# A 4096 x 4096 Strassen-like matmul on one core: the fourth product of seven regions in quarters, and A's rows measured on ScalarE

## The chip, the cores and the metric

The kernel runs on one core of a Trainium2 chip. The metric is the device time of one execution in microseconds (us); lower is better. The core's engines each follow their own instruction list in order: TensorE (PE in the profile; its weight loads are PEld), VectorE (DVE), ScalarE (ACT), GpSimd (POOL) and SyncE (SP). POOL, SP and ACT also issue DMA transfers.

## What is computed

```python
def reference(a, b, alpha):          # a, b: 4096 x 4096 float32, alpha = 0.01
    x = np.matmul(a, b)
    return np.where(x > 0, x, alpha * x)
```

The kernel multiplies in float16 with float32 sums and replaces eight block products by seven, in the manner of Strassen and Winograd. Because the sums of blocks lose accuracy where rows of A or columns of B differ much in size, it also sums the squares of every row of A and every column of B ("measures" them). At the end it looks at the largest, the smallest and the total, and a plain branch in bfloat16 computes the product again if they are too uneven. On this input that branch isn't taken.

## The kernel before, in words

The output is cut into 4 bands `g` of 1024 rows and 4 column blocks `j` of 1024 columns; one pair is a **region**, named (g, j) here. The first region, (0,0), is computed plainly while the first data come in; the other 15 follow in the list `regions` (L487), in a band in the order 2, 0, 1, 3 (band 2: 2, 0, 3, 1; band 0: 1, 2, 3). In each, A's band and B's block are split into halves (A11 to A22, B11 to B22), and seven products of 512 x 2048 by 2048 x 512 are made. `PRODUCTS` (L622) lists them: a11, a12, s2, s3, s1, a22 and s4 are the left sides, where s1 to s4 are sums of A's blocks, made once a band. The right sides are B11, B21, T2, T3, T1, T4 and B22: VectorE makes the T's in place with `b_sum` (L569, eight of 128x4096 a region). T3 lies where B12 was, T2 and T1 where B11 was.

A whole product (`product`, L725; matmuls on L734) is 64 matmuls of 512 columns into four PSUM banks. In the ten regions of bands 1 to 3 that are not the last of a band that another band follows (`in_quarters`, L901), the sixth and the seventh product use the same scheme again one level down: seven products of a quarter each (`quarter_product`, L678, matmuls on L684), 16 matmuls of 256 columns. They need four sums of quarters of A (`sums_of_a`, made in the first region of a band, stored in DRAM and loaded in the others by `load_sums`) and four of B (`t3_of_b` and `sums_of_b`, L644 to L656, on VectorE). Of the four quarters of the left side, the third, x[1,0], is used only in such sums, never as an operand.

Around the products the order is written by hand; the text of the loop is each engine's order. In a region it is: product 0; `early.end`; the middle measure begins; `keep` copies product 0's banks to SBUF by ScalarE (L747); the four `b_sum`s for T3 and T2, with a small memset (L702) after which SP reloads the second half of s2; the middle measure ends; product 1 and its `add` (L869) and `leave` (leaky pass L307, stores L874); four `b_sum`s for T4 and T1; product 2, its `keep`, the late measures; product 3 and its `keep` into `v`; then T3 and sums for the sixth product, product 4, and so on. As `v` takes the buffers that the first block had, its copies wait for that block's stores.

A `Measure` (L212) squares four pieces of 128x2048 with ScalarE (L227) into buffers of the pool `a16` (three buffers), and VectorE adds, turns, reduces and folds them into `stats` (L236 to L260). Which block is measured where stands in `MEASURED` and `EARLY` (L611, L620). The fields of `MEASURED` are the middle measure, the late ones and two more.

B's blocks are fetched by POOL as converting DMAs (L513; column block 2 is kept in float16 and loaded by SP), each into the place of the same block of the region before, as soon as TensorE has released it: B12 after product 3, B11 after product 4, B21 in the sixth product, B22 after the seventh. In the last region of bands 0 to 2 (`turning`) the next band of A comes in: `fetch_a` (L889) has POOL fetch 16 pieces of 128 rows into `a16` buffers (L130), and VectorE turns each (`turn`, L139).

Of the kernel before, what the change touches and what calls it, by code (L numbers as in the profile page):

```python
# [8 lines left out]
P = 128  # L9
DT = mybir.dt.float16  # L10
BF16 = mybir.dt.bfloat16
# [35 lines left out]
def kernel(  # L47
# [4 lines left out]
    alpha,  # L52
    out: bass.AP,
):

# [63 lines left out]
    def load_a(row, k0, kw, tiles, to, dt=DT):  # L121

        kc = kw // P
        held = []

        def fetch():
            a16 = a16_pool.tile([P, 4 * tiles, kw // 4], dt, name="a16")
            for q in range(4):
                src = a[row:row + tiles * P, k0 + q * kw // 4:k0 + (q + 1) * kw // 4]
                nc.gpsimd.dma_start(a16[32 * q:32 * q + 32], src.rearrange("(g i) w -> i g w", i=32))  # L130
            held.append(a16)

        def turn(t0=0, t1=tiles):
            parts = to(t0, t1)
            n = kc // 2 // len(parts)
            src = (held[0][:, 4 * t0:4 * t1, :].rearrange("p g w -> p (g w)").bitcast(U32)
                   .rearrange("p (g j c) -> p g c j", j=32, c=kc // 2))
            for i, part in enumerate(parts):
                nc.vector.transpose(  # L139
                    part.rearrange("p c m e -> p c (m e)").bitcast(U32)  # L140
                    .rearrange("p c (g i) -> p g c i", i=32),
                    src[:, :, i * n:(i + 1) * n, :],
                )

        return fetch, turn

    def pieces_a(g, h, u, urgent=False):
# [423 lines left out]
    def measure(i, which, x, y, room=None):  # L571
# [7 lines left out]
            return MeasureFirst(which, parts, None)  # L579
        return Measure(which, parts, not which, room)  # L580

    def judge(line):


        ends = small_pool.tile([P, 3, 2], FP32, name="ends")
        for n, op in enumerate((MAX, MIN, ADD)):
            nc.vector.tensor_reduce(ends[:, n], stats[:, n], axis=X, op=op)
        lines = dram_pool.tile([P, 6], FP32, name="lines")
        nc.sync.dma_start(lines, ends.rearrange("p n w -> p (n w)"))
        nc.sync.dma_start(line, lines.rearrange("p k -> (p k)").rearrange("(o k) -> o k", o=1))  # L590
        yield
        by = line.rearrange("o (p n w) -> o n w p", n=3, w=2)
        most, least, total, ok, more = (
            small_pool.tile([1, 2], FP32, name=name) for name in ("most", "least", "total", "ok", "more"))
        for t, n, op in ((most, 0, MAX), (least, 1, MIN), (total, 2, ADD)):
            nc.vector.tensor_reduce(t, by[:, n], axis=X, op=op)
        nc.vector.tensor_scalar(more, least, EVEN, None, op0=MULT)
        nc.vector.tensor_tensor(ok, most, more, LE)
        for t, limit, op in ((most, GREATEST, LE), (least, LEAST, GE), (total, 1e30, LE)):
            nc.vector.tensor_scalar(more, t, limit, None, op0=op)  # L600
            nc.vector.tensor_tensor(ok, ok, more, MULT)
        good = small_pool.tile([1, 1], I32, name="good")
        nc.vector.tensor_tensor(good, ok[:, :1], ok[:, 1:], MULT)
        yield good
# [3 lines left out]

    A11, A12, A22 = (0, 0, 0), (0, 0, 1), (0, 1, 1)
    B11, B12, B21, B22 = ((1, half, nt) for half in range(2) for nt in range(2))  # L610
    MEASURED = {  # L611
        (0, 1): (None, [A11], B12, B11), (0, 2): (B21, [B22, A22], B12, A12),
        (1, 0): (A12, [B22], None, None), (1, 1): (A22, [A11], None, None),
        (2, 0): (B21, [A12], None, None), (2, 3): (A22, [A11], None, None),
        (3, 0): (A12, [A22], None, None),
        (3, 1): (B21, [B22], None, None), (3, 3): (B21, [B22], None, None),
    }


    EARLY = {(1, 1): B11, (2, 0): B11, (2, 3): B11, (3, 0): B12, (3, 1): B12, (3, 3): A11}  # L620

    PRODUCTS = [("a11", 0, 0), ("a12", 1, 0), ("s2", 0, 0), ("s3", 0, 1), ("s1", 0, 0), ("a22", 1, 0), ("s4", 1, 1)]  # L622


    HALF = NT // 2
    QUARTER = KC * HALF
    kept_s2 = dram_pool.tile([2, P, KC * RM], DT, name="kept_s2")
    kept_q = {name: dram_pool.tile([4, P, QUARTER], DT, name=f"kept_q{name}") for name in ("a22", "s4")}
    side = 0

    def a_quarter(t):
# [26 lines left out]
    def sums_of_a(g, name, room):  # L658

        x = {key: q.rearrange("p c m e -> p c (m e)") for key, q in quarters_of_a(g, name).items()}  # L660
        made = {}

        def make(n, x0, x1, op):
            made[n] = room(n)
            f = lambda t: made[t].rearrange("p (c m) -> p c m", m=2 * HALF) if isinstance(t, int) else x[t]
            nc.vector.tensor_tensor(f(n), f(x0), f(x1), op)
            nc.sync.dma_start(kept_q[name][n - 1], made[n])

        make(1, (1, 0), (1, 1), ADD)
        make(2, 1, (0, 0), SUB)  # L670
        make(3, (0, 0), (1, 0), SUB)
        make(4, (0, 1), 2, SUB)

    def load_sums(name, to, which, queue=nc.sync):
        for n in which:
            queue.dma_start(to[n], kept_q[name][n - 1])
# [18 lines left out]
    def new_a16(_=None):  # L695
        return a16_pool.tile([P, QUARTER], DT, name="q16", tag="a16")
# [18 lines left out]
    for i, (g, j) in enumerate(regions):  # L715
# [28 lines left out]
        def keep(banks, side):  # L744
            pairs, kept = new_c(side)
            for mt in range(MT):
                nc.scalar.copy(kept[mt], banks[mt])  # L747
            return pairs, kept

        def sixth_in_quarters(pairs, banks, v, y, tq, sq):  # L750

# [135 lines left out]
                    coming[h, half] = next_a(g + 1, h, half)  # L887

        def fetch_a(h, half, some=slice(None)):  # L889
            if turning:  # L890
                for fetch, turn in coming[h, half][some]:
                    fetch()
                    turn()

        y = [new_bank(ybank + mt) for mt in range(MT)]
        z = [new_bank(zbank + mt) for mt in range(MT)]
# [2 lines left out]
        late_ones = [measure(i, *x) for x in late_ones]  # L899
        first_of_group = i == 0 or regions[i - 1][0] != g  # L900
        in_quarters = g > 0 and not turning  # L901
        early = measure(i, *EARLY[g, j]) if (g, j) in EARLY else None
        if early:
            early.begin()
        if first_of_group and g:
            keep_s2(g)

        product(0, y, True)
        if early:
            early.end()  # L910
        if middle:
            middle.begin()
        have_t2 = g > 1 and j == CACHED
        if have_t2:
            for k in ks:
                t = have_b[i, k, 0] = b_pool.tile([P, KC, NT], DT, name="b", tag="b11")
                move_t("t2", t, k, False, nc.scalar)
        _, u1 = keep(y, side)
        for k in ks:
            if have_t2:  # L920
                break
            b_sum(B(0, 1, k), B(1, 1, k), B(0, 1, k), SUB)
            if late_s2 and k == ks[0]:
                load_s2(g, ks[1], True)
            b_sum(B(0, 0, k), B(0, 1, k), B(0, 0, k), ADD)
            if g == 1 and j == CACHED:
                move_t("t3", B(0, 1, k), k, True)
                move_t("t2", B(0, 0, k), k, True)
        if middle:
            middle.end()  # L930
        if first_of_group:
            sum_a(g, "s3")
            if g:
                sum_a(g, "s4")
# [4 lines left out]
        leave(u1, 0, 0)  # L939
        if g:  # L940
            fetch_a(0, 0, slice(3, None))
        for k in ks:
            b_sum(B(1, 0, k), B(1, 0, k), B(0, 0, k), SUB)
        if first_of_group and g:
            sums_of_a(g, "s4", new_a16)
        if not g:
            fetch_a(0, 1)

# [5 lines left out]
            b_sum(B(0, 0, k), B(1, 1, k), B(0, 0, k), SUB)  # L954
        if g:
            fetch_a(0, 1)
        if i == 0:
            sum_a(g, "s4")
        if late_ones:
            late_ones[0].end()  # L960
        if in_quarters:
            t = x_pool.tile([P, 4, QUARTER], DT, name="q", tag="x")
            tq, sq = {2: t[:, 0], 1: t[:, 1], 4: t[:, 2]}, {4: t[:, 3]}
        if in_quarters and first_of_group:
            sums_of_a(g, "a22", lambda n: sq.setdefault(n, sq[4] if n == 4 else new_a16()))
        elif in_quarters:
            for n in (1, 2, 3):
                sq[n] = new_a16()
            load_sums("a22", sq, (1, 2, 3, 4))

        z = [new_bank(zbank + mt) for mt in range(MT)]
        product(3, z, True)
        _, v = keep(z, side)
        fetch_b(i + 1, [(0, 1)], ks)
        fetch_a(1, 0)
        for m in late_ones[1:]:
            m.begin()
            m.end()
# [10 lines left out]
                good = next(judged)  # L989

        product(4, y, False)
        a21 = None
        if turning:
            new_s(g + 1, "s1")
            t = new_s(g + 1, "s2").rearrange("p k c m e -> p (k c m e)").bitcast(BF16)
            a21 = measure(i + 1, 0, 1, 0, t.rearrange("p (n w) -> p n w", n=4))
            a21.begin()
        if in_quarters:
            tq, sq = sixth_in_quarters(u2_pairs, [new_bank(zbank + mt) for mt in range(MT)], v, y, tq, sq)
        else:  # L1000
            add(v, y)
            leave(v, 1, 1)
        if a21:
            a21.end()
        if fifth:
            fifth = measure(i + 1, *fifth)
            fifth.begin()
# [105 lines left out]
```

## Time and profile before

| | |
|---|---|
| median of 3 runs | 1552.65 us (1552.44 to 1552.97) |
| the profiled execution | 1552.24 us, of which its span, first to last instruction, is 1550.1 us |
| TensorE busy (share of the span) | 1537.9 us (99%) |
| VectorE | 1154.6 us (74%) |
| ScalarE | 374.2 us (24%) |
| GpSimd | 300.4 us (19%) |
| DMA moved | 329.68 MB, mean 213 GB/s |
| granted TensorE clock, mean | 0.998 |
| chain of work that ended last | PE 96%, DMA 2%, DVE 1%, POOL 1%, issue 1% |

A busy share is a mean over stages; TensorE's 99% says that it has nearly always a matmul under way, not which wait would end last if the others changed. That is read from the timelines of single regions. In the lists, `x4` counts instructions, `[1.62 <-ACT c L819]` is the idle time of that engine before them and what ended it, and the DMA share is the busy time of the 16 DMA engines over the stretch (transfers overlap in one engine, so it can exceed 1).

### The profile page before, as it was taken

Reading aid. Unit: us, or ns where it says so; the run is one execution under the profiler, and the core shown is the slowest. Engines: PE = TensorE matmul, PEld = TensorE weight load, DVE = VectorE, ACT = ScalarE, POOL = GpSimd, SP = SyncE. Lnnn points to the kernel's source line nnn. Section 1 sums busy time; section 2 is a strip of 40 time slices with the busy share of each in tenths; the row PEclk is TensorE's granted clock in tenths of the full one; section 3 lists DMA queues with packets and bytes.
Section 4 is the critical chain, followed back from the end, with each engine's and each line's share of the span. In section 5 each row is a group of like instructions: output and inputs, shape, how many; then the busy total and the mean of one; then the engine's idle time right before and its main releaser. Section 6 shows DMA issues by size and latency. Waiting matters only on the chain.

```text
span 1550.1 us, 20720 instructions
## 1 busy us (share of the span) xinstructions
PE 1537.9 (99%) x8235; PEld 804.8 (52%) x8235; DVE 1154.6 (74%) x1315; ACT 374.2 (24%) x394; POOL 300.4 (19%) x482
## 2 busy tenths in 40 slices
PE   9999999999999999999999999999999999999997
PEld 4444444444447456474444746547444464745646
DVE  4368758777996586966699588685879769678696
ACT  2201243612110324300121141430021143051430
POOL 5641110144002011023400202012340110201100
PEclk9999999999999999999999999999999999999999
DMA  9999694999869889499996959969998894969923
GB/s 246 186 216 194 135 286 153 181 202 192 271 253 259 188 177 277 113 273 219 184 339 207 270 141 229 233 145 278 215 213 314 198 277 101 276 166 193 287 82 139
DMA packets 210092, 329.68 MB, mean 213 GB/s; under 512 B 18497, under 2 KB 155969, under 8 KB 202050
## 3 DMA queue, kind: packets, MB, share of 16 engines
q0 software_dynamic: 149376, 141.59, 57.4%
q1 hardware_dynamic: 53986, 161.12, 27.9%
q10 hardware_dynamic: 6624, 25.56, 4.4%
q8 instruction: 66, 1.08, 0.3%
q14 instruction: 40, 0.33, 0.1%
HBM read 369.10 MB, written 98.57 MB: 302 GB/s over the span
## 4 chain that ended last, share of the span: by engine, by line
PE 96%; DMA 2%; DVE 1%; POOL 1%; issue 1%; ACT 0%; SPq 0%; DVEq 0%
PE ps L734 76%; PE ps L684 16%; PE ps L279 4%; DMA b<-in_b_dram 1%; DVE a L139 1%; DMA a<-in_a_dram 0%; POOL a L130 0%; DMA a_in<-in_a_dram 0%; POOL b L189 0%; DVE part L318 0%; PE turned L366 0%; DVE part L314 0%; DVE c L860 0%; DVE c L307 0%; DVE a L373 0%
## 5 line engine op out<-in xcount | busy, mean ns | idle before, releaser
L734 PE MATMUL ps<-b,a 128*128 128x512 f16 x3200 | 696.4, 379 | 0.0
L734 PEld LDWEIGHTS <-a 128*128 128x128 f16 x3200 | 313.2, 98 | 375.6
L734 PE MATMUL ps<-b,s 128*128 128x512 f16 x2240 | 489.2, 379 | 0.0
L734 PEld LDWEIGHTS <-s 128*128 128x128 f16 x2240 | 219.1, 98 | 264.3
L513 POOL DMA_DIRECT2D b<-in_b_dram x184 | 136.6, 747 | 927.3 <-PE ps L734 582.9
L569 DVE TENSOR_TENSOR b<-b 128x4096 f16<-128x4096 f16 x104 | 234.7, 2289 | 91.3 <-DMA b<-in_b_dram 88.1
L747 ACT COPY c<-ps 128x512 f32<-128x512 f32 x180 | 92.7, 598 | 457.0 <-PE ps L734 381.9
L139 DVE STREAM_TRANSPOSE a<-a 128x512 uint32<-128x512 uint32 (+2 forms) x120 | 126.8, 1103 | 82.4 <-DMA a<-in_a_dram 79.7
L130 POOL DMA_DIRECT2D a<-in_a_dram x252 | 137.8, 553 | 196.2 <-DVE a L139 112.6
L307 DVE SCALAR_TENSOR_TENSOR c<-c 128x512 f32<-128x512 f32 x240 | 149.6, 687 | 3.1 <-ACT c L1042 3.0
L227 ACT ACTIVATE sq<-b 128x2048 bf16<-128x2048 f16 x64 | 119.2, 1911 | 107.5 <-DVE sq L236 91.1
L869 DVE TENSOR_TENSOR c<-ps,c 128x512 f32<-128x512 f32 x142 | 88.8, 682 | 67.7 <-PE ps L734 57.5
L684 PEld LDWEIGHTS <-q 128*128 128x128 f16 x1280 | 125.2, 98 | 14.5
L279 PE MATMUL ps<-b,a 128*128 128x512 f16 x512 | 112.9, 379 | 2.0 <-DVE part L318 0.9
L227 ACT ACTIVATE sq<-a 128x2048 bf16<-128x2048 f16 x48 | 89.1, 1911 | 102.2 <-DVE sq L236 81.0
L279 PEld LDWEIGHTS <-a 128*128 128x128 f16 x512 | 49.7, 98 | 63.1 <-issue 3.4
L684 PE MATMUL ps<-b,q 128*128 128x256 f16 x640 | 74.8, 273 | 0.0
L810 ACT COPY c<-ps 128x512 f32<-128x512 f32 x9 | 5.3, 588 | 253.1 <-PE ps L684 225.0
L763 DVE TENSOR_TENSOR c<-ps,c 128x512 f32<-128x512 f32 x80 | 52.3, 686 | 14.5 <-PE ps L684 14.5
L684 PE MATMUL ps<-q,q 128*128 128x256 f16 x480 | 57.3, 273 | 0.0
L684 PEld LDWEIGHTS <-a 128*128 128x128 f16 x480 | 47.0, 98 | 7.6
L684 PEld LDWEIGHTS <-s 128*128 128x128 f16 x480 | 47.0, 98 | 5.4
(100 smaller groups left out, 769.7 us busy)
## 6 DMA issues: line engine op xcount, KB each, us to landing
b<-in_b_dram POOLq DMA_DIRECT2D x192, 512.0 KB, 13.1
out_dram<-c SPq DMA_DIRECT2D x240, 256.0 KB, 6.2
a<-in_a_dram POOLq DMA_DIRECT2D x244, 128.0 KB, 5.4
b<-kept SPq DMA_DIRECT2D x20, 1024.0 KB, 8.7
q<-kept_qs ACTq DMA_DIRECT2D x40, 512.0 KB, 8.2
s<-kept_s SPq DMA_DIRECT2D x18, 1024.0 KB, 7.3
q<-kept_qa SPq DMA_DIRECT2D x28, 512.0 KB, 6.0
b<-in_b_dram POOLq DMA_DIRECT2D x24, 256.0 KB, 9.1
```

What stands on the lines that cost most here:

```text
L130: nc.gpsimd.dma_start(a16[32 * q:32 * q + 32], src.rearrange("(g i) w -> i g w", i=32))
L139: nc.vector.transpose(part.rearrange("p c m e -> p c (m e)").bitcast(U32) .rearrange("p c (g i) -> p g c i", i=32), src[:, :, i * n:(i + 1 ...
L227: nc.scalar.activation(to, self.parts[n], SQUARE)
L279: nc.tensor.matmul(ps, a_cols(at[0, h, u], c, mt, (h, u) == (0, 0)), bt[0, u, nt][:, c, :], start=first, stop=last,)
L307: nc.vector.scalar_tensor_tensor(t, t, alpha, t, op0=MULT, op1=MAX if alpha <= 1 else MIN)
L513: nc.gpsimd.dma_start(t[:, c:c + 4, :], b_rows(j, u, c, 4, nt, g > 0))
L569: nc.vector.tensor_tensor(f(to), f(x0), f(x1), op)
L684: nc.tensor.matmul(to[m], xq[:, c // 2, rows, c % 2], yq[:, c, :], start=first and c == 0 and m < banks, stop=c == KC - 1, skip_group_chec ...
L734: nc.tensor.matmul(banks[mt], a_cols(t, c, mt, t is first_a), B(half, nt, k)[:, c, :], start=first and (k, c) == todo[0], stop=(k, c) == t ...
L747: nc.scalar.copy(kept[mt], banks[mt])
L763: nc.vector.tensor_add(block, pair(t), block)
L869: nc.vector.tensor_add(to, bank, to)
```

## The change

In seven regions, all those in quarters but the first of a band (`in_fourth`), the fourth product (index 3, s3 times T3) is made in quarters too. Its sums of B's quarters are made by VectorE before the second pair of `b_sum`s. Its sums of A's quarters are made in the second region of a band (`sums_of_s3`) and lie where the quarters x[1,0] of a22, s4 and s3 were (`x21`), with the third of them in the `q` tile. They are also stored in DRAM, and loaded again in the third and fourth region. The displaced quarters are stored in DRAM (`keep_x21`, bands 1 and 2) and brought back in the turning region, where the whole products need them (`load_x21`).

The blocks of A in bands 1 to 3 are no longer measured by `Measure`. As each piece comes in, ScalarE squares its four strips and sums along them (`square_rows`), and VectorE folds 16 numbers a block into `stats` (`note_rows`). The measures of B that remain are placed anew; the middle measure now begins after `keep`. The core of the diff:

```diff
+    def square_rows(piece, n, to):
+        for q in range(4):
+            nc.scalar.activation(junk, piece[:, q, :], SQUARE, accum_out=to[:, 4 * n + q:4 * n + q + 1])
+    def note_rows(but=0):
+        while len(rows_made) > but:
+            r = rows_made.pop(0)
+            for n, op in enumerate((MAX, MIN, ADD)):
+                nc.vector.tensor_tensor(stats[:, n, 0], stats[:, n, 0], r, op)
...
+    EARLY = {(1, 0): B11, (1, 1): B11, (2, 0): B12, (2, 3): B11, (3, 1): B12}
...
-        (1, 0): (A12, [B22], None, None), (1, 1): (A22, [A11], None, None),
-        (2, 0): (B21, [A12], None, None), (2, 3): (A22, [A11], None, None),
-        (3, 0): (A12, [A22], None, None),
-        (3, 1): (B21, [B22], None, None), (3, 3): (B21, [B22], None, None),
+        (1, 1): (B21, [], None, None), (2, 0): (B22, [], None, None),
+        (3, 0): (B21, [], None, None), (3, 3): (B21, [], None, None),
     }
-    EARLY = {(1, 1): B11, (2, 0): B11, (2, 3): B11, (3, 0): B12, (3, 1): B12, (3, 3): A11}
+    IN_ROOM = {(1, 3): B22, (2, 1): B22}
...
+    def x21(g, name):
+        return operand(g, name, 0)[:, :, HALF:, :]
+    def keep_x21(g, name):
+        if g < G - 1:
+            nc.sync.dma_start(by_chunk(kept_x21[name]), by_chunk(x21(g, name)))
+    def load_x21(room, kept):
+        for c in range(KC // 2):
+            nc.sync.dma_start(by_chunk(room)[:, c], by_chunk(kept)[:, c])
+    def sums_of_s3(g, rooms):
+        x = {key: by_chunk(q) for key, q in quarters_of_a(g, "s3").items()}
+        sx = {n: by_chunk(room) for n, room in rooms.items()}
+        sx[3] = by_chunk(new_a16())
+        for n, x0, x1, op in ((1, x[1, 0], x[1, 1], ADD), (3, x[0, 0], x[1, 0], SUB),
+                              (2, sx[1], x[0, 0], SUB), (4, x[0, 1], sx[2], SUB)):
+            nc.vector.tensor_tensor(sx[n], x0, x1, op)
+            nc.sync.dma_start(by_chunk(kept_q["s3"][n - 1]), sx[n])
...
+        def fourth_in_quarters(banks, tq, sx):
+            pairs, kept = new_c(side)
+            b = quarters_of_b(i, 0, 1)
+            x = quarters_of_a(g, "s3")
+            one, other, third, fourth = banks
+            t = lambda n: b_quarter(tq[n])
+            block = lambda r, n: pairs[r][:, :, n * HALF:(n + 1) * HALF]
+            def more(r, n, bank):
+                nc.vector.tensor_add(block(r, n), pair(bank), block(r, n))
+            quarter_product(x[0, 1], b[1, 0], into(fourth), True)
+            quarter_product(x[0, 0], b[0, 0], into(one), True)
+            nc.scalar.copy(block(0, 0), pair(one))
+            more(0, 0, fourth)
+            quarter_product(sx[4], b[1, 1], into(other), True)
+            nc.scalar.copy(block(0, 1), pair(other))
+            quarter_product(x[1, 1], t(4), into(third), True)
+            nc.scalar.copy(block(1, 0), pair(third))
+            quarter_product(sx[2], t(2), into(one))
+            more(0, 1, one)
+            quarter_product(sx[1], t(1), into(fourth), True)
+            nc.scalar.copy(block(1, 1), pair(fourth))
+            more(0, 1, fourth)
+            quarter_product(sx[3], b[0, 1], into(one))
+            more(1, 0, one)
+            more(1, 1, one)
+            return kept
...
         def fetch_a(h, half, some=slice(None)):
...
+                fetch, turn = coming[h, half][n]
+                fetch()
+                turn()
+                square_rows(turn.held[0], n, coming["rows", h, half])
...
+        in_fourth = in_quarters and not first_of_group
+        second_of_group = in_fourth and regions[i - 2][0] != g
+        if in_fourth:
+            rooms = {1: x21(g, "a22"), 2: x21(g, "s4"), 4: x21(g, "s3")}
...
+        if second_of_group:
+            keep_x21(g, "s3")
...
         product(0, y, True)
         if early:
             early.end()
-        if middle:
-            middle.begin()
+        if second_of_group:
+            sums_of_s3(g, rooms)
...
         _, u1 = keep(y, side)
+        if middle:
+            middle.begin()
...
         if middle:
             middle.end()
+        if in_fourth and not second_of_group:
+            for n in (1, 2, 4):
+                load_x21(rooms[n], kept_q["s3"][n - 1])
+        if g and turning:
+            for name in ("s3", "a22", "s4"):
+                load_x21(x21(g, name), kept_x21[name])
...
+        if in_fourth:
+            tq = {n: new_a16() for n in (2, 4, 1)}
+            t3_of_b(quarters_of_b(i, 0, 1))
+            sums_of_b(quarters_of_b(i, 0, 1), tq)
         for k in ks:
             b_sum(B(1, 0, k), B(1, 0, k), B(0, 0, k), SUB)
...
+        if in_fourth:
+            v = fourth_in_quarters(z, tq, {**rooms, 3: a_quarter(t[:, 3])})
+            sq = {n: t[:, 3] if n == 4 else new_a16() for n in (1, 2, 3, 4)}
             load_sums("a22", sq, (1, 2, 3, 4))
+        else:
+            product(3, z, True)
+            _, v = keep(z, side)
...
-        a21 = None
+        in_room = None
         if turning:
...
-            a21 = measure(i + 1, 0, 1, 0, t.rearrange("p (n w) -> p n w", n=4))
-            a21.begin()
+            if (g, j) in IN_ROOM:
+                in_room = measure(i, *IN_ROOM[g, j], t.rearrange("p (n w) -> p n w", n=4))
+                in_room.begin()
```

## The prediction

> **What bounds the kernel now.** I read the chain of work that ended last first, then VectorE's timeline in one region, then the DMA shares over stretches of that region, then the groups. The chain, in order of time (start, us, what):
>
> ```profile
> 1423.82 24.45 PE ps L684 x224
> 1448.28 69.07 PE ps L734 x320
> 1517.34 23.59 PE ps L684 x216
> 1541.03 0.70 DVE c L860
> ```
>
> From 123.13 us to 1541.03 it is TensorE alone: no other engine ends a wait there. A region in quarters takes 69.07 + 24.45 = 93.52 us, and two rates can be read: 320 matmuls of 512 columns in 69.07 us (215.8 ns each, a whole product of 64 is 13.81 us), 224 of 256 columns in 24.45 us (109.15 ns each, one quarter product of 16 is 1.746 us, seven are 12.22 us). So fewer matmul columns are worth their full time, as long as every operand and bank is ready. Whether they are is read from VectorE, here in the last region, (3,3), which starts at 1448.28 (start, us, line, what; idle time before in brackets):
>
> ```profile
> 1466.06 2.29 DVE L569 TENSOR_TENSOR b<-b 128x4096 f16<-128x4096 f16 x1 [4.13 <-DMA b<-in_b_dram]
> ...
> 1471.12 4.69 DVE L569 TENSOR_TENSOR b<-b 128x4096 f16<-128x4096 f16 x2 [0.38 <-DMA b<-in_b_dram]
> 1475.73 1.22 DVE L236 TENSOR_TENSOR sq<-sq 128x2048 bf16<-128x2048 bf16 x1
> ...
> 1482.84 2.48 DVE L869 TENSOR_TENSOR c<-ps,c 128x512 f32<-128x512 f32 x4
> 1485.23 2.49 DVE L307 SCALAR_TENSOR_TENSOR c<-c 128x512 f32<-128x512 f32 x4
> 1487.63 8.89 DVE L569 TENSOR_TENSOR b<-b 128x4096 f16<-128x4096 f16 x4
> 1496.44 1.22 DVE L236 TENSOR_TENSOR sq<-sq 128x2048 bf16<-128x2048 bf16 x1
> ```
>
> Measured from the region's start: B22 lands in two halves, at 17.8 and 22.8; the sums for T2 end at 27.45; the middle measure takes 7.11, the adds of the second product 2.39, the leaky pass 2.40, four b_sums 8.81, to 48.16. VectorE has no gap from 22.8 to there, while TensorE is elsewhere: this hidden chain, started by a DMA, is what the change lengthens. The DMA engines (stretch, sums of busy time, clock 1.00, then DMA share and GB/s):
>
> ```profile
> 1454.00:1463.00 9.00, 9.00 (x43) 4.04 (x42) 6.98 (x10) 6.92 (x5) 0.00 (x0) 1.00 1.18 256
> 1463.00:1469.00 6.00, 6.00 (x29) 2.72 (x28) 2.85 (x3) 3.24 (x5) 0.00 (x0) 1.00 1.25 207
> 1473.00:1486.00 13.00, 13.00 (x62) 5.91 (x61) 11.97 (x18) 7.43 (x4) 0.00 (x0) 1.00 0.01 1
> ```
>
> They are full until B22 has landed and idle after: bytes added before that moment delay it.
>
> **The change, part by part.** *Seven fourth products* (bands 1 to 3, all regions but the first and a turning one) go from 64 x 215.8 ns to 112 x 109.15 ns: 13.81 - 12.22 = 1.59 us each, **-11.1 us**. The sixth and seventh products already run at that spacing, so I give this no range.
>
> *A new wait.* The fourth product reuses two banks: its sixth quarter product overwrites the bank of its first, which VectorE must have added by then. That add stands behind everything above in VectorE's order, and TensorE is in order, so all later matmuls wait. The sixth quarter starts at 3 x 13.81 + 5 x 1.746 = 50.16. Before it, VectorE now also has t3 and three sums of B12's quarters (four ops of L646 to L656, 1.22 each; in region (1,1) the same four ran from 656.56 to 661.35, 4.79). The add itself is 0.69 (L763). In a region with a middle measure: 48.16 + 4.79 + 0.69 = 53.64, **a stall of 3.5 us**, over twice what that region gains. Four of seven have one: (1,1), (2,0), (3,0), (3,3). Without it the adds start when the second product ends, at 27.62: 27.62 + 2.39 + 2.40 + 4.79 + 8.81 + 0.69 = 46.7, 3.4 to spare: (1,0), (2,3), (3,1). The late A measures that go stand behind the b_sums and come too late to help. ScalarE's copy that the fifth quarter waits for is ready at about 44.92 + 0.6 of 48.41 (L747, 598 ns); it costs nothing unless the first block's store lands after 47.8.
>
> *More DMA while B22 lands.* The second region of a band, (1,0), (2,0), (3,0), stores s3's four sums and, in bands 1 and 2, the displaced quarter, 0.5 MB each: 2.5 MB (2.0 in band 3), on SP, whose next entry is the reload of s2. The page prices SP's queue:
>
> ```profile
> q1 hardware_dynamic: 53986, 161.12, 27.9%
> ```
>
> 27.9% of 1550.1 us over 161.12 MB is 2.68 us a MB when nothing shares. So B22 is 6.7 (5.4) us late; bounds: nothing, if the stores land after it, and 9.4 with the 1 MB reload ahead too. I take 6.7, because the stores are issued from about 7 to 18 and the engines are full to 22. In band 1 and 2, a22's quarter, stored in the region before while it is full as well, adds 1.35. [...]
>
> Past T2 the chain is 2.39 + 2.40 + 4.79 + 8.81 + 0.69 = 19.08, plus 7.11 with a measure; T2 ended at 27.58, 27.54 and 27.19 there.
> (1,0): 27.58 + 6.7 + 1.35 + 19.08 - 50.16 = 4.6.
> (2,0): 27.54 + 8.05 + 7.11 + 19.08 - 50.16 = 11.6.
> (3,0): 27.19 + 5.4 + 7.11 + 19.08 - 50.16 = 8.6.
> (1,1): 3.5, plus up to 2 from 1.5 MB of reloads issued as B22's second half lands, less what (1,0)'s stall gives the DMA engines: 0 to 5.5, taken as 2.
> (3,3): the same without a stall ahead of it: 4.5. (2,3), (3,1): 0.
> Stalls: 4.6 + 11.6 + 8.6 + 2 + 4.5 = **31.3 us**. The sums of s3 themselves (4 x 1.22) lie in the wait for B22.
>
> *The rows by ScalarE.* 192 squares of 128x512 replace 48 of 128x2048; each between a quarter of L227's 1911 ns (0.48) and 0.78 (L747's 598 ns and a small op of 0.17); I take 0.65, near L747: 2.6 a piece. VectorE loses twelve A measures of some 7 us, none on the path above. But ScalarE is in order: in a turning region the copies of the fourth product now stand behind the squares of the fourth piece of A's second block, and the sixth product needs them at 5 x 13.81 = 69.05. That piece:
>
> ```profile
> 758.02 2.10 DVE L139 STREAM_TRANSPOSE a<-a 128x512 uint32<-128x512 uint32 x2 [7.21 <-DMA a<-in_a_dram]
> ```
>
> It lands 64.25 after (1,3) started (693.77): 64.25 + 2.6 + 2.06 (four copies) = 68.9, nothing to spare; in (2,1) 1.1 more. The 1.5 MB that restore the three quarters (4.0 us) come ahead of A's pieces. So 0 to 6 each; I take 2.5, two regions, **5 us**. (0,3) has that piece at 47.2 and no reloads: 0. Folding the rows costs 0.35 a time, in place of the same in the measures.
>
> *The clock.* The last matmul ends at 1541.80; in the stretch 1545 to 1549 the granted clock averages 0.52, so it falls to half at 1545.16, 3.4 us later. The first 11 matmuls (L103) took 4.78 us, 435 ns each: half speed costs 4.78 - 11 x 0.216 = 2.4 us until it rises. The stalls of (2,0) and (3,0) are long enough: **4.8 us**; bounds 0 and five times 2.4. [...]
>
> Sum: -11.1 + 31.3 + 5 + 4.8 = +30.0. The profiled execution took 1552.24 (span 1550.1 and 2.1 around it; median of the runs 1552.65): **1582 us**.
>
> **Rivals.** *B, only the order costs*: the stores don't delay B22, and ScalarE keeps up: 4 x 3.5 - 11.1 = +2.9, 1555. For: the stores finish late in the window. Against: the shares over 1. *C, faster*: B22 lands some 3.5 us earlier in the measured regions than it did, since TensorE's shorter regions and fewer VectorE measures let the loads be issued earlier; then the add ends by 50.16 everywhere and 1541 remains. It decides at T2's end: 23.9 or sooner. Against: loads are issued on TensorE's progress, and the space between their release and the region's end is 45 us before and after. *D, worse*: each turning region loses 6, (1,0) 6.5, (1,1) 5.5, (2,0) 14, (3,0) 11, (3,3) 6, and the clock falls five times: -11.1 + 43 + 12 + 12 = +56, 1608. That quarters don't run at half a matmul is excluded by the 24.45 us rows.
>
> **Chances.** Forecast 0.62, B 0.18, C 0.09, D 0.11. The range takes in the bounds from B up to nearly D: 1555 to 1606. A measurement of this kernel can tell 0.2% (3.1 us) from no change. Faster by more is C: 0.09. Within 0.2% is half of B, 0.09. Slower: 0.82.
>
> **What would show it.** Right: TensorE idles before the sixth quarter of the fourth product, released by VectorE's add, 3 to 5 us in (3,3), more in (2,0) and (3,0); B22's first b_sum there later than 17.8; a clock under 1.00 after. Wrong: no gap in TensorE's chain, or B22 landing as before, or VectorE's add ahead of its four b_sums.

## The result, and the profile after

| | before | after |
|---|---|---|
| median (lowest to highest) | 1552.55 us (1551.76 to 1553.1, 6 runs) | 1587.8 us (1585.16 to 1590.55, 6 runs) |
| the profiled execution, span | 1552.24, 1550.1 us | 1589.72, 1587.8 us |
| granted clock, mean | 0.998 | 0.989 |
| VectorE, ScalarE busy | 1154.6, 374.2 us | 1148.6, 425.7 us |

The changed kernel is slower: 1.0229 times the time before, 95% interval 1.0216 to 1.0242. In its profile a whole product's matmuls are on L775, the quarters' on L725, `b_sum` on L571, the fourth product's adds on L801, the second product's add on L940, the sums of B's quarters on L662 to L672, the squares of A's rows on L590.

The waits of TensorE (what waited for what: us in total, times, longest us) name the loss at once; before, no such wait was there:

```profile
PE ps L725 <- DVE c L801: 23.4, 5, 6.9
PE ps L725 <- DVE c L940: 4.9, 2, 2.4
PE ps L775 <- DVE b L571: 4.6, 4, 2.2
```

The first line is the new wait, in the five regions (1,0), (1,1), (2,0), (3,0) and (3,3): a quarter product that may not start before VectorE's add. The other two are in the second regions of the bands only: the first quarter of the fourth product waits for the bank that VectorE's add of the second product empties, and product 2 (the third one) waits for the sums of T2. Two groups and SP's queue from the page (count, then busy us, mean ns, idle before):

```profile
L590 ACT ACTIVATE junk<-a 128x512 bf16<-128x512 f16 x192 | 121.4, 632 | 104.3 <-DMA a<-in_a_dram 99.1
L725 PE MATMUL ps<-q,a 128*128 128x256 f16 x384 | 52.4, 296 | 24.0 <-DVE c L801 23.4
...
q1 hardware_dynamic: 73714, 183.67, 31.8%
```

SP moved 22.55 MB more. A square of a strip takes 632 ns, but ScalarE starts one only every 0.76 us, since a small instruction that reads out its sum stands behind each; the prediction took 0.65, and its upper bound was 0.78:

```profile
759.35 0.63 ACT L590 ACTIVATE junk<-a 128x512 bf16<-128x512 f16 x1
759.89 0.19 ACT L590 ACTIVATION_READ_ACCUMULATOR junk<-a 128x1 f32 x1
```

The chain, in order of time, is no longer TensorE alone. In the last region, (3,3):

```profile
1481.13 41.44 PE ps L775 x192
1522.57 8.75 PE ps L725 x80
...
1532.07 2.29 DVE b L571
1534.35 0.61 DVE c L801
...
1535.01 6.25 PE ps L725 x32
```

Three products run without a gap, then five quarters (80 matmuls), and then the chain leaves TensorE: the last of the four `b_sum`s, one add, the last two quarters. Those 32 matmuls take 6.25 us where 3.5 is their full speed. VectorE's timeline of the same stretch shows why it was late (the region starts at 1481.0):

```profile
1504.16 4.69 DVE L571 TENSOR_TENSOR b<-b 128x4096 f16<-128x4096 f16 x2 [0.34 <-DMA b<-in_b_dram]
1508.77 1.22 DVE L238 TENSOR_TENSOR sq<-sq 128x2048 bf16<-128x2048 bf16 x1
...
1515.87 2.48 DVE L940 TENSOR_TENSOR c<-ps,c 128x512 f32<-128x512 f32 x4
...
1520.67 1.23 DVE L662 TENSOR_TENSOR b<-b 128x2048 f16<-128x2048 f16 x1
...
1525.46 8.89 DVE L571 TENSOR_TENSOR b<-b 128x4096 f16<-128x4096 f16 x4
1534.27 1.28 DVE L801 TENSOR_TENSOR c<-ps,c 128x512 f32<-128x512 f32 x2
```

B22's second half, 23.2 us after the region's start as before (23.0); the measure; the adds; the new sums of B's quarters; the four `b_sum`s; and only then the add. From the first line to the last VectorE is idle only once, 0.65 us inside the measure, as before the change. TensorE had asked for it at 1531.3.

By region, what the time lost is made of (gaps of TensorE; and slower matmuls, which is the region's excess over an undisturbed one less its gaps):

| region | B22's second half, before and after | gaps predicted | gaps | slower matmuls |
|---|---|---|---|---|
| (1,0) | 23.1, 31.1 | 4.6 | 4.3 | 0.3 |
| (1,1) | 23.4, 23.0 | 2 | 3.5 | 2.9 |
| (2,0) | 23.1, 32.6 | 11.6 | 12.4 | 2.4 |
| (3,0) | 22.8, 31.0 | 8.6 | 9.6 | 3.9 |
| (3,3) | 23.0, 23.2 | 4.5 | 3.7 | 2.8 |
| (2,3), (3,1) | 23.3, 22.7 and 23.8, 22.5 | 0 | 0 | 0 |
| sum | | 31.3 | 33.5 | 12.3 |

With -11.1 for the quarters, 2.5 for the two turning regions (1.23 and 1.27 longer, with the region after them) and 0.6 at the two ends this is +37.8; the profiled spans differ by 37.7.

### The profile page after: what moved, and what is told of

Same layout as the page of the kernel before. It is cut to its first block, busy times and chain, and to the rows that moved or that the text cites. A ratio compares the mean times of both kernels' runs of the same rounds, so it can differ in the third digit from the quotient of the medians.

```text
span 1587.8 us, 21919 instructions
## 1 busy us (share of the span) xinstructions
PE 1539.4 (97%) x8571; PEld 842.4 (53%) x8571; DVE 1148.6 (72%) x1318; ACT 425.7 (27%) x730; POOL 300.4 (19%) x482
## 5 line engine op out<-in xcount | busy, mean ns | idle before, releaser
L775 PE MATMUL ps<-b,a 128*128 128x512 f16 x2752 | 599.5, 379 | 1.3 <-DVE c L940 0.7
L775 PE MATMUL ps<-b,s 128*128 128x512 f16 x2240 | 489.7, 379 | 4.6 <-DVE b L571 4.6
L775 PEld LDWEIGHTS <-a 128*128 128x128 f16 x2752 | 269.1, 98 | 325.4 <-issue 2.8
L775 PEld LDWEIGHTS <-s 128*128 128x128 f16 x2240 | 219.1, 98 | 268.1 <-issue 5.0
L571 DVE TENSOR_TENSOR b<-b 128x4096 f16<-128x4096 f16 x104 | 234.7, 2289 | 104.1 <-DMA b<-in_b_dram 100.0
L788 ACT COPY c<-ps 128x512 f32<-128x512 f32 x152 | 79.0, 597 | 424.2 <-PE ps L775 408.0
L590 ACT ACTIVATE junk<-a 128x512 bf16<-128x512 f16 x192 | 121.4, 632 | 104.3 <-DMA a<-in_a_dram 99.1
L725 PEld LDWEIGHTS <-q 128*128 128x128 f16 x1392 | 137.5, 99 | 17.3
L940 DVE TENSOR_TENSOR c<-ps,c 128x512 f32<-128x512 f32 x142 | 88.9, 683 | 62.0 <-PE ps L775 54.1
L725 PEld LDWEIGHTS <-a 128*128 128x128 f16 x1040 | 105.5, 101 | 49.3 <-issue 30.5
L229 ACT ACTIVATE sq<-b 128x2048 bf16<-128x2048 f16 x56 | 104.5, 1913 | 92.3 <-DVE sq L238 63.3
L281 PE MATMUL ps<-b,a 128*128 128x512 f16 x512 | 112.8, 379 | 2.9 <-DMA b<-in_b_dram 1.8
L725 PE MATMUL ps<-b,q 128*128 128x256 f16 x752 | 90.4, 277 | 0.0
L281 PEld LDWEIGHTS <-a 128*128 128x128 f16 x512 | 49.7, 98 | 63.9 <-issue 4.9
L725 PE MATMUL ps<-b,a 128*128 128x256 f16 x656 | 77.6, 276 | 4.9 <-DVE c L940 4.9
L881 ACT COPY c<-ps 128x512 f32<-128x512 f32 x9 | 5.3, 588 | 269.7 <-PE ps L725 149.4
L725 PE MATMUL ps<-q,a 128*128 128x256 f16 x384 | 52.4, 296 | 24.0 <-DVE c L801 23.4
```

The costliest lines, as they stand in the source:

```text
L229: nc.scalar.activation(to, self.parts[n], SQUARE)
L281: nc.tensor.matmul(ps, a_cols(at[0, h, u], c, mt, (h, u) == (0, 0)), bt[0, u, nt][:, c, :], start=first, stop=last,)
L571: nc.vector.tensor_tensor(f(to), f(x0), f(x1), op)
L590: nc.scalar.activation(junk, piece[:, q, :], SQUARE, accum_out=to[:, 4 * n + q:4 * n + q + 1])
L725: nc.tensor.matmul(to[m], xq[:, c // 2, rows, c % 2], yq[:, c, :], start=first and c == 0 and m < banks, stop=c == KC - 1, skip_group_chec ...
L775: nc.tensor.matmul(banks[mt], a_cols(t, c, mt, t is first_a), B(half, nt, k)[:, c, :], start=first and (k, c) == todo[0], stop=(k, c) == t ...
```

## The experiments

The theory on trial is that of the prediction: the quarters give their 1.59 us a region, and one wait, a quarter for an add that stands behind all else in VectorE's order, takes it back and more, most where the added stores make B22 late. Its rivals: the time is lost to the amount of DMA traffic, to ScalarE's squares, or to VectorE being late for everything, so that another wait would stand there if this one went.

**The rows alone.** `in_fourth` is false everywhere, with no displaced quarters stored or loaded; what stays is A's rows on ScalarE and the measures at their new places.

```diff
-        in_fourth = in_quarters and not first_of_group
+        in_fourth = False
...
```

> Only the second half of the change: A's rows squared by ScalarE, measures placed as in the changed kernel, no fourth product in quarters, no displaced quarters, no s3 sums. Theory: nothing on TensorE's path but ScalarE's copies in the turning regions, 0 to 2.5 us: 1552.5 to 1555. Rival (the rows are what costs: squares delay ScalarE's copies and A's buffers): 1558 or more.

Measured: 1552.95 us (1551.6 to 1553.73, 11 runs), ratio 1.000 (0.9991 to 1.0009). The squares and the new places cost nothing that can be measured. The whole loss is the fourth product's.

**No middle measures.** The four middle measures of bands 1 to 3 are left out (their columns of B are then not measured).

```diff
-        (1, 1): (B21, [], None, None), (2, 0): (B22, [], None, None),
-        (3, 0): (B21, [], None, None), (3, 3): (B21, [], None, None),
```

> The changed kernel without the four middle measures (column blocks B21 of j = 0, 1 and 3 and B22 of j = 0 are not measured; the rest is computed as before). Theory (VectorE's order: the fourth product's first add stands behind 7.1 us of measure and four b_sums, with B22's landing as the start of that chain): (1,1) and (3,3) lose nothing instead of 6.3 and 6.5, (2,0) some 5.5 instead of 14.8, (3,0) some 3 instead of 13.5, (1,0) 4.6 as it was; about 1555, and at most one fall of the clock. Rival (the added transfers alone do it, the measures run in time that is waited anyway): all five regions still stall, 1580 or more.

Measured: 1563.63 us (1561.47 to 1565.36, 4 runs), ratio 1.0071 (1.0055 to 1.0086). (1,1) and (3,3) have no stall left, as expected. The second regions keep 5.0 to 5.7 us of gaps each, 3.20 of it at the sixth quarter, and the clock fell three times; I had expected 4.6, 5.5 and 3. The miss of 8.6 us is 3 us of gaps, above all in (3,0), whose B22 is as late as in the others (32.4 after its start), and three stretches of 3.41 us at half speed, 5.1 us (the granted clock is 0.996 in the mean).

**No reloads of s3's sums.** The stores of sums 1, 2 and 4, which only the reloads need, and the reloads are left out: 1.5 MB less ahead of B22 in the second regions, 1.5 MB less in each later one.

```diff
-            nc.sync.dma_start(by_chunk(kept_q["s3"][n - 1]), sx[n])
+            if n == 3:
+                nc.sync.dma_start(by_chunk(kept_q["s3"][n - 1]), sx[n])
...
-        if in_fourth and not second_of_group:
-            for n in (1, 2, 4):
-                load_x21(rooms[n], kept_q["s3"][n - 1])
```

> The changed kernel without the stores of s3's first, second and fourth sum and without their reloads in the third and fourth region (they still lie where they were made). Theory (transfers ahead of B22 are worth 2.68 us a MB): B22's second half lands 4 us earlier in (1,0), (2,0) and (3,0); (1,0) loses about 0.6, (2,0) 10.8, (3,0) 8, (1,1) and (3,3) nearly what they lost; about 1573. Rival (only VectorE's order costs, the stores finish too late to matter): no landing moves by more than 1 us, 1585 to 1588.

Measured: 1573.56 us (1572.6 to 1578.06, 4 runs), ratio 1.0132 (1.0117 to 1.0148). In the profiled execution, the slowest of the four (1578.06 us), B22's second half came 3.8, 5.1 and 6.6 us earlier in (1,0), (2,0) and (3,0): 2.5 to 4.4 us for each MB taken away from ahead of it. (1,1) and (3,3) kept their stalls (3.7 and 4.2 us), so the reloads are no part of those.

**Another order on VectorE.** The four `b_sum`s for T4 and T1, which products 4 and 5 need, stand behind the adds of the fourth product that TensorE waits for, two behind the first add and two behind the second; nothing is left out. `t4_and_t1(k)`, not shown, makes the two of one half `k`.

```diff
         for k in ks:
-            b_sum(B(1, 0, k), B(1, 0, k), B(0, 0, k), SUB)
+            if not in_fourth:
+                b_sum(B(1, 0, k), B(1, 0, k), B(0, 0, k), SUB)
...
             more(0, 0, fourth)
+            t4_and_t1(ks[0])
...
             more(0, 1, one)
+            t4_and_t1(ks[1])
```

> The changed kernel with the four b_sums for T4 and T1 behind the fourth product's first add (two) and second bank's add (two) in VectorE's order, nothing else. Theory: no wait for the first add is left in (1,1) and (3,3) (12.8 us less); (1,0) keeps its 1.3 in the third product; in (2,0) and (3,0) the late landing and the middle measure still hold the second product's adds, 6.3 and 4.5 in place of 14.8 and 13.5; about 1554. Rival (the b_sums are only moved in front of product 4, which then waits for T1): product 4 starts 2 us or more late in each of the seven regions, 1565 or more.

Measured: 1558.53 us (1556.88 to 1560.03, 5 runs), ratio 1.0036 (1.0023 to 1.0049): 29 us of the 35 are gone by order alone. (1,1) and (3,3) run without a gap and product 4 isn't late. What is left is in the second regions, whose B22 is as late as ever (31.1 to 32.3): 2.0, 5.1 and 5.7 us of gaps, in product 2 and the first four quarters but for 1.5 us at the seventh quarter of (2,0) and of (3,0), which waits for the second add, behind two of the moved `b_sum`s.

**The stores moved.** The same bytes at other times: X21 of s3 goes out a region earlier, beside s4's, and the stores of s3's sums behind the sums for T3 and T2, hence behind the reload of s2.

```diff
-        if second_of_group:
-            keep_x21(g, "s3")
...
             keep_x21(g, "s4")
+            keep_x21(g, "s3")
...
-            nc.sync.dma_start(by_chunk(kept_q["s3"][n - 1]), sx[n])
+        return sx
...
-        if in_fourth and not second_of_group:
+        if second_of_group:
+            for n in (1, 3, 2, 4):
+                nc.sync.dma_start(by_chunk(kept_q["s3"][n - 1]), sx3[n])
+        elif in_fourth:
```

> The changed kernel with the same transfers at other times: the 0.5 MB store of S3's X21 goes out in the first region of a group (beside S4's), and the four stores of S3's sums go out in the second region behind the T3 and T2 sums of B, so that only what the kernel before also had stands ahead of B22's second half. Theory (the added transfers make B22 late in the second regions, and the order of VectorE's work does the rest): B22's second half is back at about 23 us after the start of (1,0), (2,0) and (3,0), from 31.0 to 32.6; (1,0)'s stalls go from 4.3 to 0, (2,0) and (3,0) keep about the 3.5 us of stall and the clock's 2.8 that (1,1) and (3,3) have, and these two keep theirs: -11.1 + 4 x 6.3 + 3.1 for turning, start and end = +17, 1570 us (1564 to 1574). Rival (the bytes, not their place, set the landing, since the stores of one region and the loads share the same DMA engines): landing at 28 or later, 1580 or more.

Measured: 1569.57 us (1568.61 to 1573.48, 4 runs), ratio 1.0113 (1.0096 to 1.013). The sums that wait for B22's second half in (2,0), on VectorE's timeline, first the changed kernel (region from 893.45), then this one (from 886.01):

```profile
926.01 4.69 DVE L571 TENSOR_TENSOR b<-b 128x4096 f16<-128x4096 f16 x2 [4.67 <-DMA b<-in_b_dram]
```

```profile
910.52 4.69 DVE L571 TENSOR_TENSOR b<-b 128x4096 f16<-128x4096 f16 x2 [0.45 <-DMA b<-in_b_dram]
```

32.6 us after the start became 24.5; in (1,0) 24.6, in (3,0) 23.1. So it is the place of the stores, not their amount. (1,0) has no gap left, and product 2 none anywhere. The four regions with a middle measure keep 3.8, 6.8, 5.4 and 3.8 us at the sixth quarter. I had expected 3.5 for (2,0) and (3,0) also. In (2,0) B22 is 1.4 us later than it was before the change, and the measure has a wait of 1.98 us more for a square of ScalarE's; in (3,0) it has the same wait of 1.98 us. That the total came out as forecast is partly luck: the ends of the run and the turning regions were some 3 us cheaper than assumed.

**Other banks.** The wait itself is taken away, and neither VectorE's order nor any transfer is touched: ScalarE's copies, not VectorE's adds, now free every bank that a later quarter uses.

```diff
             quarter_product(sx[4], b[1, 1], into(other), True)
-            nc.scalar.copy(block(0, 1), pair(other))
             quarter_product(x[1, 1], t(4), into(third), True)
             nc.scalar.copy(block(1, 0), pair(third))
             quarter_product(sx[2], t(2), into(one))
-            more(0, 1, one)
-            quarter_product(sx[1], t(1), into(fourth), True)
-            nc.scalar.copy(block(1, 1), pair(fourth))
-            more(0, 1, fourth)
+            nc.scalar.copy(block(0, 1), pair(one))
+            more(0, 1, other)
+            quarter_product(sx[1], t(1), into(third), True)
+            nc.scalar.copy(block(1, 1), pair(third))
+            more(0, 1, third)
```

> The changed kernel with other banks in the fourth product and nothing else: the sixth quarter starts in the bank of the fourth quarter, which ScalarE's copy has emptied, and ScalarE, not VectorE, reads the first bank before the seventh quarter adds to it; so no quarter waits for VectorE any more, though VectorE does the same adds as late as before. Theory (the stall is this one wait, not the late data as such): the fourth product's stalls (3.2, 3.5, 6.9, 6.1, 3.7 us in (1,0), (1,1), (2,0), (3,0), (3,3)) go with the clock falls behind them; product 2's stay (1.1, 5.5, 3.5), and product 4 is late by 0.5 to 2.7 in (2,0) and (3,0) only, since its own B sums end only 0.7 us ahead of the add that the stall waited for: -11.1 + 10.1 + 3.1 + 1 to 7 = +3 to +9, 1556 to 1562 us. Rival (VectorE is late for everything, so that the next product takes the whole stall over): 1575 or more.

Measured: 1558.15 us (1554.37 to 1559.78, 8 runs), ratio 1.0033 (1.0022 to 1.0043). TensorE's timeline in (3,3), first the changed kernel, then this one:

```profile
1529.39 1.91 PE L725 MATMUL ps<-q,s 128*128 128x256 f16 x16
1535.01 3.57 PE L725 MATMUL ps<-q,a 128*128 128x256 f16 x16 [3.71 <-DVE c L801]
1538.37 2.88 PE L725 MATMUL ps<-b,q 128*128 128x256 f16 x16
```

```profile
1503.60 1.91 PE L725 MATMUL ps<-q,s 128*128 128x256 f16 x16
1505.35 1.91 PE L725 MATMUL ps<-q,a 128*128 128x256 f16 x16
1507.09 1.91 PE L725 MATMUL ps<-b,q 128*128 128x256 f16 x16
1508.84 3.40 PE L775 MATMUL ps<-b,s 128*128 128x512 f16 x15
```

and VectorE's in the second, at the same place:

```profile
1500.47 8.89 DVE L571 TENSOR_TENSOR b<-b 128x4096 f16<-128x4096 f16 x4
1509.28 3.27 DVE L801 TENSOR_TENSOR c<-ps,c 128x512 f32<-128x512 f32 x5
```

The adds run as late as ever, from 54.1 us after the region's start (53.3 in the changed kernel); the sixth quarter starts 3.9 us before the first of them, and the next product follows without a gap. In (1,1) and (3,3), whose B22 is not late, only this one wait depended on VectorE, and no gap is left. The second regions keep 1.4, 4.6 and 3.6 us in product 2 and the first four quarters. (In the changed kernel the 16 matmuls of the quarter after the wait took 3.4 us, here 1.75; that is the clock, granted at 0.51 from 1533.5 to 1540.4, below.) In (2,0), product 4 then waits 0.59 us for its B sum, at the low end of what was expected.

**Both causes removed, in two ways.** The stores moved, with the other order, and the stores moved, with the other banks.

> The stores moved as in the run beside it, and the four B sums of T4 and T1 put behind the first add of the fourth product as in the run on the order alone (1558.5). Theory: no stall is left in the fourth products, and none in product 2, since B22 lands at 23: -11.1 + 2.5 (turning regions) + 0.6 (start and end) = -8, 1545 us (1542 to 1549), below the kernel before. Rival (the late half of B22 is not from the stores): (2,0) and (3,0) keep their 5 us each and (1,0) its 2, 1556 to 1559 as without the move.

> The other banks and the moved stores together, VectorE's order untouched and all measures in place. Theory: with B22 at 23 us product 2 is not late, no quarter waits for VectorE, and product 4 finds its B sums made: -11.1 + 3.1 = -8, 1545 us (1542 to 1549), the same as by the order. Rival (VectorE's late adds come back at product 4 or in the sixth product, whose sums of B stand behind them): 1550 to 1560, with the wait shown at product 4 or at the sixth product's first sum.

Measured: 1546.35 us (1546.25 to 1546.96, 5 runs), ratio 0.996 (0.9946 to 0.9975), by the order; 1544.49 us (1543.84 to 1548.53, 4 runs), ratio 0.9955 (0.9939 to 0.9972), by the banks. Both are faster than the kernel before, by 0.4 and 0.45%, and do all its work. In the second, the waits of TensorE in and right behind the fourth product have shrunk to

```profile
PE ps L775 <- DVE b L571: 0.6, 1, 0.6
PE ps L725 <- DVE q L670: 0.5, 1, 0.5
```

Of the six regions with the fourth product in quarters that another one follows, all but (2,0) (93.38) take 91.93 us, where each took 93.52 before, and the clock never falls inside the run (0.999 in the mean). 8.4 us of the 11.1 are kept (1552.86 less 1544.49); 1.5 go in (2,0) and 1.3 in the turning regions.

## Why the prediction held, step by step

The forecast was 1582 us, +30.0 against the profiled execution; it came to +37.5 there, and +35.3 between the medians, inside the range, and by the mechanism that was named. Its errors partly cancel: the clock was taken 7.5 us too low and the stalls 2.2, the turning regions 2.5 too high.

- *The gain*: 1.59 us a region. The three products and the fourth in quarters take 53.67 us in the undisturbed (2,3) and (3,1), where 4 x 13.81 would be 55.24. Right, and shown again by the 91.93 us above.
- *The new wait*: right in its place, its releaser and its five regions. The run with other banks removes it and nothing else and gains 29.7 us; the run with another order removes its cause and gains 29.3. What the prediction didn't name is that 10.1 of the 33.5 us fall earlier: T2's sums end 35.7 to 37.3 us into the second regions, and the second half of product 2 wants them at 2.5 x 13.81 = 34.5, so it waits too (1.1, 5.5 and 3.5 us, together with the first four quarters). The place of the sixth quarter is not changed by that: T2's measured end and the forecast's chain behind it (19.08, and 7.11 with a measure) put it at 54.8, 63.5 and 61.9, and it started at 54.8, 63.4 and 61.9.
- *B22 late by the stores*: T2's sums were to end at 35.6, 35.6 and 32.6 us into (1,0), (2,0), (3,0); they ended at 35.7, 37.3 and 35.7. The lateness in (3,0) was taken 3 us too small. What SP's queue moved there from the region's start until B22 had landed, before and after the change (packets, MB, share of 16 engines):

```profile
q1 hardware_dynamic: 776, 2.52, 31.2%
q1 hardware_dynamic: 2594, 5.24, 49.1%
```

That is 2.7 MB more: the stores, which had all landed 29.4 us into the region, and more of the 1 MB reload of s2, which I had kept out of the sum and which landed at 31.9, right behind B22 (30.9). In (1,0) it is 2.4 MB more and in (2,0) 2.9, and B22 landed 7.9, 9.5 and 8.3 us later: 3.0 to 3.3 us a MB, where 2.68 was taken. That (3,0)'s gaps came out only 1.0 us above the forecast is luck: the clock fell before the sixth quarter there, and 2.1 us of slower matmuls, most of them at half clock (0.50 for 3.41 us), stand in place of a gap. The stores on SP's queue, moved, gave POOL's load 6.5 to 8.1 us back, so here the one queue's transfers did hold up the other's.
- *(1,1)*: the step that let (1,0)'s stall relieve the DMA engines, 2 us in place of 3.5, was wrong. B22 landed at 23.0 there, neither earlier for the stall nor later for the reloads; the gap was 3.5, the sum of the order alone.
- *ScalarE in the turning regions*: 5 us taken, 2.5 measured, and not by the squares: in the run with the rows alone the same squares are there, and those regions are 0.5 and 0.2 us longer. In the changed kernel the sixth product, where the wait was expected, starts without one in both. The first matmuls of (2,1)'s fourth product wait 1.28 us in all for VectorE's add of the second product,

```profile
PE ps L775 <- DVE c L940: 0.7, 3, 0.2
```

(three gaps of 0.22 us; the starts of these matmuls lie 1.28 us further apart than at full speed). The other 1.2 us are at the start of (2,2), the region behind (1,3): 0.57 for its first block of B, which in the run with the rows alone is 0.5 as well, and 0.66 for ScalarE's copies of (1,3)'s last product. Over the runs a turning region is 0 to 2.6 us longer, and why it varies is open.
- *The clock*: the term that was mis-sized, 4.8 taken, some 12 measured. I let it fall only in the two regions with long stalls, at 2.4 us each; that the others were too short was my estimate. It fell five times, in (1,1), (2,0), twice in (3,0) and in (3,3), so the stall of 3.5 us in (1,1) was enough. The upper bound that I gave, five times 2.4, is what happened.

Of the rivals, the one by which only the order costs (1555) is refuted by B22's landing. The one that ends faster was wrong for this kernel, since B22 did not come earlier in the measured regions; but its number, 1541, is what the change is worth without its two waits, and the last run comes within 4 us of it. The worse one (1608) had the clock's five falls right, and the stalls (43) and the turning regions (12) too high.

## What to carry to other kernels

When a product is cut into parts that reuse a bank, look at who empties it: a reader that stands at the end of a long in-order list makes TensorE wait for the whole list, and an engine with little before it (here ScalarE, with as many copies as before) frees the bank with no wait at all here. Place new stores behind the load that the critical engine's helper waits for; the same bytes made it 7.9 to 9.5 us late ahead of it, and 0.4 to 1.5 behind it. And price a stall with the clock that falls after it: here 12 us on top of 33.

## What the runs showed of the hardware

In the changed kernel the clock fell at shorter stalls than I had thought: at gaps of 2.44, 3.46 and 3.71 us in (3,0), (1,1) and (3,3), besides the long ones of 6.89 and 6.13 in (2,0) and (3,0). Stretches of the changed kernel (sums of busy time: PE, PEld, DVE, ACT, POOL, then the granted clock), around the stall of (3,3) and then that of (1,0):

```profile
1530.10:1533.50 3.40, 1.20 (x11) 0.93 (x10) 3.40 (x2) 0.08 (x1) 0.00 (x0) 1.00 0.72 270
1533.50:1540.40 6.90, 5.39 (x26) 3.86 (x26) 2.75 (x4) 0.59 (x1) 0.00 (x0) 0.51 0.17 65
1540.40:1543.80 3.40, 3.40 (x21) 1.88 (x20) 2.51 (x6) 0.00 (x0) 0.00 (x0) 1.00 0.61 217
```

```profile
557.30:560.70 3.40, 1.49 (x14) 1.18 (x13) 3.40 (x2) 0.37 (x1) 0.00 (x0) 1.00 1.16 185
560.70:564.10 3.40, 2.11 (x20) 1.89 (x20) 1.84 (x3) 0.17 (x1) 0.00 (x0) 1.00 1.09 306
```

With TensorE busy 1.20 of 3.40 us the clock was half (0.51) for the next 6.9; with 1.49 of 3.40 it stayed at 1.00, though that stall was nearly as long (3.20 us against 3.71). In the changed kernel's record of the granted clock the five falls inside the run lie whole multiples of 3.413 us apart (87, 110, 4 and 56 of them). Counted in stretches of that length back from the falls, TensorE was idle for 2.21 to 3.28 us of the stretch before each of the five, and the stall of (1,0) is cut into 1.93 and 1.27 us; no stretch at full clock with up to 1.93 us idle was followed by a fall. The clock was back at 1.00 after one stretch in one case, the first in (3,0), where TensorE was idle for 0.14 us of it, and after two in the other four, where it was idle for 1.25 to 3.41 us of the first. Of two equal gaps in that kernel, the one in (3,0) (2.44 us, 2.30 of it in one stretch) was followed by a fall, and the one in (2,0) (2.43 us, cut into 1.78 and 0.66) was not. In the run with other banks the gap of 2.43 us in (3,0) was again followed by half clock (0.50 over the next 3.4 us), and that in (2,0) was not: the 48 matmuls after it took 5.40 us, their full speed.
